# Moving twelve gate tiles from one attention stage to the next, and a branch one stage later

## The chip, the cores and the metric

The kernel runs on one core of a Trainium2 chip, as one program. A core has five engines that each take their own instructions in order: TensorE (matrix products), VectorE, ScalarE, GpSimd and SyncE, which here only starts transfers. They wait for each other on semaphores. The metric is the time of one execution in microseconds. Before the change it is 3099.02 us, the median of three runs (3095.4 to 3099.54).

## The reference

Two blocks follow each other. The first one (a recurrent branch, an attention with a learned selection, a mixture of experts) isn't touched. The second one runs two layers over 512 tokens of width 1024. What matters of a layer is this:

```
proj = x @ w_in[l]           # 3 x 512 for NA, 3 x 512 for DF, 384 + 256 + 32 for MLA, 3 x 1024 gate columns
na_out  = neighbourhood_attention(na_q, na_k, na_v, na_rpb[l])          # 8 heads of 64
df_out  = diff_attention(df_q, df_k, df_v, ...)                         # 4 heads, two score maps each
mla_out = latent_attention(m_cq, m_ckv, m_kr, w_mla_qb[l], w_mla_kvb[l], ...)   # 8 heads
    # inside: rms_norm(c_q), rms_norm(c_kv) over the 384 and 256 columns, then the products by w_qb and w_kvb
gates = sigmoid(gate_pre + b_gate[l])                                   # (512, 3, 1024)
merged = gates[:, 0] * (na_out @ w_branch[l, 0]) + gates[:, 1] * (df_out @ w_branch[l, 1]) \
       + gates[:, 2] * (mla_out @ w_branch[l, 2])
x = layer_norm(ALPHA * x + merged @ w_out[l]); x = layer_norm(ALPHA * x + ffn(x))
```

The gates depend on the layer's input alone; branch 0 needs na_out and its gates, branch 1 df_out, branch 2 mla_out.

## The kernel before

Every product with a weight is done in three matmuls: the weight block is loaded as `raw`, ScalarE casts it to a rounded copy `wh`, VectorE writes the rest `wl = raw - wh` (both in `split`, L145 and L146), and TensorE adds wh and wl products (`mmk`, L298, L299, L301). A tile of the class `FM` gives 128 output features of all 512 tokens in one PSUM accumulator `fm`; with 8 pieces of the input it takes 24 matmuls of 512 columns. There are four such accumulators (`mm`), three buffers for transposes and scores (`tr`) and one for the attention's output (`po`).

A gate (`gate`, L1638 ff.) is one such tile, a sigmoid on ScalarE (`bg`) and a store to DRAM (`t_d`); there are 3 x 8 in a layer. A branch (`branch`) has eight tiles of 12 matmuls; each multiplies its accumulator with a loaded gate (`tl`, L1656), and branches 1 and 2 add what the one before stored (`ml`, L1660 on GpSimd).

A layer goes through three attention stages. In each, `weave` interleaves two generators step by step, in the ratio of two numbers: an attention, whose chain of scores, softmax, transposes and products leaves TensorE idle, and a stream of independent work (the filler).

- NA stage: 16 units (`na_score`, `na_av`, `na_products`). A unit's scores are 4 matmuls (`nas`); VectorE adds the bias (L1589), takes the maximum (L1591, L1592), ScalarE does two sigmoids (L1595), VectorE scales (`naP`, L1601); one step later TensorE transposes (`napt`, L1607), the result is split, and again one step later come 12 products (`nao`). At each fourth unit two tiles project a head pair's queries and keys (`naq`, `nak`). Filler before: 20 gates.
- DF stage: 20 steps of scores (`dfs`), transposes (`dfpt`) and products (`dfo`), with a norm per head (a ones' matmul `dfm`). Filler before: four gates, the projection of the latent queries (`mcq`, four accumulators at once), one tile of branch 0, that of the latent keys (`mckv`, four accumulators), a tile of branch 0, the other six tiles, then the latent keys and values and the first half of the queries.
- MLA stage: 36 steps of scores (`ms`), transposes (`mpt`) and products (`mo`). Filler: the second half of the queries, branch 1.

Then branch 2 and the output projection. The functions `ev_cq` and `ev_ckv` empty the accumulators of the two latent projections: statistics on the PSUM tile by VectorE (`rms_stat`: bn_stats, then a root on ScalarE, L192, refined by VectorE), then a copy by ScalarE with that scale (L1762, L1778, and L1780 for the rotary columns). The root and the sigmoid come from different tables of ScalarE, and each change is a table load.

The order of instructions on each engine isn't quite that of the code: a scheduler of the framework moves them within what their dependences allow.

## Time and profile before

| | us |
|---|---|
| three runs, median | 3099.02 |
| profiled execution | 3100.77 |
| its span | 3098.6 |
| TensorE busy | 2908.0 (94%) |
| VectorE busy | 1840.3 (59%) |
| ScalarE busy | 1131.2 (37%) |

The span is the time from the first to the last instruction. TensorE's busy time is the sum of overlapping pipelined durations, so 94% doesn't mean that it is at its peak: what it loses shows in the spaces between the starts of its matmuls. In the profile PE is TensorE, PEld its loading of weights, DVE VectorE, ACT ScalarE, POOL GpSimd.

### The profile page before, as it was taken

Reading aid. Unit: us, or ns where it says so; the run is one execution under the profiler, and the core shown is the slowest. Engines: PE = TensorE matmul, PEld = TensorE weight load, DVE = VectorE, ACT = ScalarE, POOL = GpSimd, SP = SyncE. Lnnn points to the kernel's source line nnn. Section 1 sums busy time; section 2 is a strip of 40 time slices with the busy share of each in tenths; the row PEclk is TensorE's granted clock in tenths of the full one; section 3 lists DMA queues with packets and bytes.
Section 4 is the critical chain, followed back from the end, with each engine's and each line's share of the span. In section 5 each row is a group of like instructions: output and inputs, shape, how many; then the busy total and the mean of one; then the engine's idle time right before and its main releaser. Section 6 shows DMA issues by size and latency. Waiting matters only on the chain.

```text
span 3098.6 us, 36572 instructions
## 1 busy us (share of the span) xinstructions
PE 2908.0 (94%) x13749; PEld 2192.0 (71%) x13749; DVE 1840.3 (59%) x3521; ACT 1131.2 (37%) x1986; POOL 279.1 (9%) x263
## 2 busy tenths in 40 slices
PE   6988999979999989999999999999999999999998
PEld 5767777743333337888877888888878876788887
DVE  6899978543332347555788644425555589764434
ACT  4555244211000114444666322223444577432221
POOL 2133000310000001211002100000121000200000
PEclk9989999989999999999999999999999999999999
DMA  7222655769999984332244523334433233632341
GB/s 226 94 84 70 218 198 176 260 259 410 411 409 410 409 344 126 116 119 87 69 122 144 203 95 109 106 125 129 126 116 96 75 109 116 228 109 88 103 143 61
DMA packets 291648, 534.17 MB, mean 172 GB/s; under 512 B 29766, under 2 KB 172276, under 8 KB 287366
## 3 DMA queue, kind: packets, MB, share of 16 engines
q1 hardware_dynamic: 288872, 527.45, 48.9%
q0 software_dynamic: 2304, 4.20, 0.4%
q8 instruction: 110, 1.80, 0.2%
q14 instruction: 76, 0.62, 0.1%
q10 hardware_dynamic: 286, 0.09, 0.0%
HBM read 486.50 MB, written 44.38 MB: 171 GB/s over the span
## 4 chain that ended last, share of the span: by engine, by line
PE 57%; DMA 10%; DVE 6%; issue 3%; ACT 2%; POOL 1%; SPq 0%; DVEq 0%; POOLq 0%; ACTq 0%
PE fm L298 9%; PE fm L301 9%; PE fm L299 9%; DMA w<-in_moe_w_dram 6%; PE e L1385 5%; DMA w2r<-in_moe_w_dram 3%; PE ffo L301 2%; PE ffo L298 2%; PE ffo L299 2%; PE mix L298 1%; PE mix L299 1%; PE mix L301 1%; POOL tl L1660 1%; DVE wl L146 1%; PE cmb L1311 1%
## 5 line engine op out<-in xcount | busy, mean ns | idle before, releaser
L146 DVE TENSOR_TENSOR wl<-raw,wh 128x1024 fp32r<-128x1024 f32 (+3 forms) x403 | 461.8, 1147 | 317.2 <-ACT wh L145 315.8
L145 ACT CAST wh<-raw 128x1024 fp32r<-128x1024 f32 (+3 forms) x403 | 388.5, 966 | 546.5 <-PE fm L301 219.5
L298 PE MATMUL fm<-xT,wh 128*128 128x512 f32 (+1 forms) x1264 | 483.5, 385 | 0.0
L299 PE MATMUL fm<-xT,wl 128*128 128x512 f32 (+1 forms) x1264 | 481.4, 383 | 1.3 <-DVE wl L146 1.3
L301 PE MATMUL fm<-xT,wh 128*128 128x512 f32 (+1 forms) x1264 | 302.2, 381 | 0.0
L299 PEld LDWEIGHTS fm<-xT,wl 128*128 128x128 f32 x1264 | 239.5, 189 | 46.8 <-DVE wl L146 1.7
L298 PEld LDWEIGHTS fm<-xT,wh 128*128 128x128 f32 x1264 | 239.3, 189 | 45.2
L1385 PE MATMUL e<-w,xx 128*64 128x512 f32 x1024 | 256.8, 600 | 10.9 <-DMA w<-in_moe_w_dram 10.9
L301 PEld LDWEIGHTS fm<-xT,wh 128*128 128x128 f32 x1264 | 232.0, 188 | 45.6
L1385 PEld LDWEIGHTS e<-w,xx 128*64 128x64 f32 x1024 | 74.9, 137 | 157.9 <-issue 133.0
L1315 DVE TENSOR_TENSOR h<-h,cmb 128x512 f32<-128x512 f32 x128 | 80.7, 682 | 126.5 <-PE cmb L1314 126.1
L299 PE MATMUL fm<-uT,wl 128*128 128x512 f32 (+1 forms) x360 | 144.8, 402 | 3.8 <-DVE wl L146 3.8
L298 PE MATMUL fm<-uT,wh 128*128 128x512 f32 (+1 forms) x360 | 144.4, 402 | 0.0
L298 PE MATMUL ffo<-wl,hid 128*128 128x512 f32 x352 | 137.1, 390 | 0.0
L299 PE MATMUL ffo<-wh,hid 128*128 128x512 f32 x352 | 136.9, 389 | 0.0
L1385 PE MATMUL e<-w2r,hp 128*64 128x512 f32 x512 | 115.1, 596 | 10.1 <-ACT hp L1429 10.1
L1947 DVE SCALAR_TENSOR_TENSOR ffs<-ffs,fm 128x512 f32<-128x512 f32 x44 | 30.2, 687 | 139.3 <-ACT ffs L1946 139.3
L301 PE MATMUL ffo<-wh,hid 128*128 128x512 f32 x352 | 108.4, 389 | 0.0
L1949 DVE SCALAR_TENSOR_TENSOR ffs<-ffs,fm 128x512 f32<-128x512 f32 x44 | 30.2, 687 | 114.4 <-PE fm L301 114.4
L1660 POOL TENSOR_TENSOR tl<-ml,tl 128x512 f32<-128x512 f32 x32 | 47.7, 1496 | 555.1 <-DVE tl L1656 550.3
L1946 ACT ACTIVATE ffs<-fm 128x512 f32<-128x512 f32 x44 | 26.3, 598 | 188.7 <-PE fm L301 188.7
L1385 PEld LDWEIGHTS e<-w2r,hp 128*64 128x64 f32 x512 | 41.1, 136 | 73.1 <-issue 58.9
(603 smaller groups left out, 5938.0 us busy)
## 6 DMA issues: line engine op xcount, KB each, us to landing
w<-in_moe_w_dram SPq DMA_DIRECT2D x192, 512.0 KB
raw<-in_w_in_dram SPq DMA_DIRECT2D x71, 1024.0 KB
w2r<-in_moe_w_dram SPq DMA_DIRECT2D x128, 512.0 KB
raw<-in_w_ffn_in_dram SPq DMA_DIRECT2D x44, 1024.0 KB
w<-in_moe_w_dram SPq DMA_DIRECT2D x32, 1024.0 KB
raw<-in_w_mod_dram SPq DMA_DIRECT2D x42, 512.0 KB
raw<-in_w_ffn_out_dram SPq DMA_DIRECT2D x20, 1024.0 KB
raw<-in_w_out_dram SPq DMA_DIRECT2D x12, 1024.0 KB
```

Source lines behind the costliest of these rows:

```text
L145: S.copy(hi, src)
L146: (eng or V).tensor_tensor(lo, src, f(hi), OP.subtract)
L298: PE.matmul(ps, l[0], r[1], start=start and n == 0, stop=False)
L299: PE.matmul(ps, l[1], r[0], start=False, stop=False)
L301: PE.matmul(ps, l[0], r[0], start=False, stop=stop and n == len(pairs) - 1)
L1311: mm = PE.matmul(ps, pl, yl[:, cs], start=True, stop=False)
L1315: V.tensor_tensor(h1[i][m], h1[i][m], ps, OP.add)
L1385: mm = PE.matmul(ps[hs], lhs[:, hs], rhs[h], start=start, stop=stop)
L1660: G.tensor_tensor(th, m, th, OP.add)
L1946: S.activation(s, pgt, AF.Tanh, scale=0.5)
L1947: V.scalar_tensor_tensor(s, s, 1.0, pgt, OP.add, OP.mult)
L1949: V.scalar_tensor_tensor(s, s, 0.5, pup, OP.mult, OP.mult)
```

## The change

In both layers the NA stage keeps only the eight gates of branch 1. The other sixteen form a stream `rest`, of which four come first in the DF stage, two during each pause behind a latent projection, two between them and six behind them. Branch 0 goes into the MLA stage, ahead of branch 1. The two evacuations copy the accumulator first, and take the statistics and scale on the copy.

```diff
--- before.py
+++ after.py
@@ -1757,14 +1757,16 @@
             chat = []
 
             def ev_cq(i, ps):
-                r = rms_stat(ps, 384, 1e-6)
                 c = sg("cq", 384)
-                S.activation(c, ps, AF.Copy, scale=r)
+                S.copy(c, ps)
+                r = rms_stat(c, 384, 1e-6)
+                V.tensor_scalar(c, c, r, None, OP.mult)
                 chat.append(c)
 
             yield from dense_tm_g(xT, w_in2, 3072, 384, ev_cq, "mcq")
-            next(filler)
-            yield
+            for _ in range(2):
+                next(filler)
+                yield
             lat["cqT"] = affine_pages(chat, col["qng"][:, 3 * l:3 * l + 3], None, "cqT")
 
         def mla_project_kv(filler):
@@ -1773,15 +1775,17 @@
             lat0["krt"] = krt
 
             def ev_ckv(i, ps):
-                r = rms_stat(ps[:, 0:256], 256, 1e-6)
                 c = sg("ckv", 256)
-                S.activation(c, ps[:, 0:256], AF.Copy, scale=r)
+                S.copy(c, ps[:, 0:256])
+                S.copy(krt[:, i * 32:(i + 1) * 32], ps[:, 256:288])
+                r = rms_stat(c, 256, 1e-6)
+                V.tensor_scalar(c, c, r, None, OP.mult)
                 chat2.append(c)
-                S.copy(krt[:, i * 32:(i + 1) * 32], ps[:, 256:288])
 
             yield from dense_tm_g(xT, w_in2, 3456, 288, ev_ckv, "mckv")
-            next(filler)
-            yield
+            for _ in range(2):
+                next(filler)
+                yield
             lat["ckT"] = affine_pages(chat2, col["kvng"][:, 2 * l:2 * l + 2], None, "ckT")
             rope_rows(krt.rearrange("p (i h d) -> p i h d", i=4, h=1), 0, 16, rope16, 1, 0, 4)
             b = trp("krt")
@@ -1900,13 +1904,14 @@
                     mla_out.append(p)
 
         mT = []
-        weave((pipelined(16, na_score, na_av, 1), 17), (chain(gates(1, 0), gates(0, 16), gates(2, 8, range(4))), 20))
+        weave((pipelined(16, na_score, na_av, 1), 17), (gates(1, 0), 8))
         for _ in df_project():
             pass
-        br0 = branch(0, na_out, 16)
+        rest = chain(gates(0, 16), gates(2, 8))
         weave((pipelined(4, df_score, df_av), 20),
-              (chain(gates(2, 8, range(4, 8)), mla_project_q(br0), mla_project_kv(br0), br0, mla_kv(), mla_q(0)), 28))
-        weave((pipelined(8, mla_score, mla_av), 39), (chain(mla_q(1), branch(1, df_out, 0)), 10))
+              (chain((next(rest) for _ in range(4)), mla_project_q(rest), (next(rest) for _ in range(2)), mla_project_kv(rest), rest,
+                     mla_kv(), mla_q(0)), 36))
+        weave((pipelined(8, mla_score, mla_av), 39), (chain(mla_q(1), branch(0, na_out, 16), branch(1, df_out, 0)), 18))
         for _ in branch(2, mla_out, 8, mT):
             pass
 
```

What stands on TensorE in the NA stage of the first layer, before, between the scores of the seventh unit (`nas_10570`) and the transposes of the sixth (`napt_10589`); `fm_10536` is the second of two whole tiles that stand behind the sixth unit's own scores:

```order
L301 MATMUL fm_10536<-xT_9636,wh_10537 128x512
L301 MATMUL fm_10536<-xT_9637,wh_10537 128x512
L301 MATMUL fm_10536<-xT_9638,wh_10537 128x512
L301 MATMUL fm_10536<-xT_9639,wh_10537 128x512
L326 MATMUL nas_10570<-nak_10380,naq_10342 128x256
L327 MATMUL nas_10570<-nak_10380,naq_10341 128x256
L326 MATMUL nas_10570<-nak_10380,naq_10342 128x256
L327 MATMUL nas_10570<-nak_10380,naq_10341 128x256
L1607 MATMUL napt_10589<-ident,naP_10475 128x128 x4
```

And of the change, the same place, where the sixth unit (number 5, counted from 0) has the scores `nas_10361`, the seventh `nas_10406`, and `napt_10425` are the sixth unit's transposes:

```order
L326 MATMUL nas_10406<-nak_10280,naq_10242 128x256
L327 MATMUL nas_10406<-nak_10280,naq_10241 128x256
L298 MATMUL fm_10446<-xT_9632,wh_10447 128x512
L299 MATMUL fm_10446<-xT_9632,wl_10448 128x512
L298 MATMUL fm_10446<-xT_9633,wh_10447 128x512
L298 MATMUL nao_10433<-napt_10385,nav_9917 64x128
L1607 MATMUL napt_10425<-ident,naP_10377 128x128 x4
L299 MATMUL nao_10433<-napt_10385,nav_9917 64x128
```

Between the sixth unit's scores and its transposes stand, in place of whole tiles, the fifth unit's four transposes, twelve products, the seventh unit's four scores, three matmuls of a gate and one product.

What stands on ScalarE in the DF stage of the first layer, before, where the four tiles of the latent queries are emptied (`rsy` is a root, `cq` the copy with its scale):

```order
L192 ACT_TABLE_LOAD
L192 ACTIVATE rsy_12500<-msq_12497 128x1
L145 CAST wh_12708<-raw_12641 128x576
L1762 ACTIVATE cq_12506<-mcq_2540_12292,rst_12502 128x384
L192 ACTIVATE rsy_12515<-msq_12512 128x1
L1762 ACTIVATE cq_12521<-mcq_2541_12299,rst_12517 128x384
L192 ACTIVATE rsy_12530<-msq_12527 128x1
L1762 ACTIVATE cq_12536<-mcq_2542_12306,rst_12532 128x384
L192 ACTIVATE rsy_12545<-msq_12542 128x1
L145 CAST wh_12738<-raw_12736 128x576
L1762 ACTIVATE cq_12551<-mcq_2543_12313,rst_12547 128x384
```

And of the change, behind the four plain copies of the accumulators:

```order
L192 ACT_TABLE_LOAD
L192 ACTIVATE rsy_12072<-msq_12069 128x1
L1642 ACT_TABLE_LOAD
L1642 ACTIVATE bg_12158<-fm_12129,cols_2951 128x512
L192 ACT_TABLE_LOAD
L192 ACTIVATE rsy_12088<-msq_12085 128x1
L145 CAST pt_12188<-dfpt_12183 128x512
L145 CAST wh_12326<-raw_12257 128x1024
L192 ACTIVATE rsy_12104<-msq_12101 128x1
L1642 ACT_TABLE_LOAD
L1642 ACTIVATE bg_12224<-fm_12195,cols_2951 128x512
L192 ACT_TABLE_LOAD
```

The roots now stand among the sigmoids of two gates, with a table load at each change, and no copy stands behind a root. In the whole program ScalarE's listing has 57 table loads against 41.

## Rows read from the trace of the kernel before

**Rows 1.** Layer 1 by stage: us, busy PE, PEld, DVE, ACT, POOL (instructions), PEclk, DMA, GB/s

```profile
1196.00:1384.15 188.15, 181.23 (x995) 153.24 (x993) 100.86 (x164) 84.63 (x153) 37.12 (x46) 1.00 0.40 127
1453.50:1597.50 144.00, 136.26 (x679) 112.48 (x677) 110.67 (x290) 92.37 (x182) 0.00 (x0) 0.98 0.31 95
1597.50:1692.50 95.00, 89.84 (x454) 68.77 (x455) 85.82 (x207) 66.96 (x143) 11.37 (x9) 0.98 0.41 122
```

**Rows 2.** Chain that ended last: start, us, what; two successive tiles

```profile
1328.05 1.81 PE fm L301 x8
1333.49 1.81 PE fm L301 x8
```

**Rows 3.** TensorE around NA unit 13: start, us, engine, line, operation

```profile
1355.60 0.28 PE L327 MATMUL nas<-nak,naq 128*128 128x256 f32 x1
1355.72 0.60 PE L1607 MATMUL napt<-ident,naP 128*128 128x128 f32 x4
1356.08 0.30 PE L298 MATMUL nao<-napt,nav 128*64 128x128 f32 x1
...
1362.89 0.49 PE L1607 MATMUL napt<-ident,naP 128*128 128x128 f32 x3
```

**Rows 4.** TensorE's waits, NA stage: us in total, times, longest

```profile
PE nas L326 <- DVE nak L311: 6.3, 4, 1.9
```

**Rows 5.** Busy time, DF stage of layer 2

```profile
2416.90:2559.80 142.90, 135.22 (x678) 111.74 (x676) 110.49 (x289) 92.45 (x182) 0.00 (x0) 0.99 0.31 96
```

**Rows 6.** VectorE around NA unit 13

```profile
1355.99 0.69 DVE L1589 SCALAR_TENSOR_TENSOR nasm<-nas,nasm 128x512 f32<-128x512 f32 x1 [1.04 <-PE nas L327]
...
1357.32 1.22 DVE L146 TENSOR_TENSOR wl<-raw,wh 128x1024 fp32r<-128x1024 f32 x1
1358.45 0.16 DVE L1592 TENSOR_SCALAR mx<-mx 128x2 f32<-128x2 f32 x1
...
1360.04 1.25 DVE L1601 TENSOR_SCALAR naP<-nasm,su 128x256 f32<-128x256 f32 x2
```

**Rows 7.** ScalarE at the same place

```profile
1355.45 0.69 ACT L1642 ACTIVATE bg<-fm,cols 128x512 f32<-128x512 f32 x1 [1.48 <-PE fm L301]
1356.04 1.04 ACT L145 CAST wh<-raw 128x1024 fp32r<-128x1024 f32 x1
```

**Rows 8.** Stretches at a low granted clock (PEclk)

```profile
1532.20:1539.00 6.80, 5.34 (x13) 4.18 (x14) 5.79 (x29) 2.06 (x9) 0.00 (x0) 0.50 0.01 4
2214.90:2218.30 3.40, 3.40 (x13) 2.72 (x11) 3.04 (x5) 0.78 (x2) 0.00 (x0) 0.50 0.66 180
2262.70:2266.10 3.40, 3.40 (x16) 3.11 (x16) 2.74 (x3) 2.23 (x3) 0.00 (x0) 0.51 0.00 0
2498.20:2501.60 3.40, 3.40 (x9) 2.65 (x8) 2.63 (x15) 1.43 (x7) 0.00 (x0) 0.50 0.00 0
```

**Rows 9.** TensorE's waits, DF stage of layer 1

```profile
PE fm L298 <- ACT krt L1780: 3.8, 1, 3.8
PE dfo L298 <- DVE pt L146: 1.3, 2, 1.1
...
PE fm L298 <- ACT cq L1762: 0.2, 1, 0.2
```

**Rows 10.** Timeline about the latent key's copies, layer 1, and TensorE in layer 2

```profile
1528.57 1.28 ACT L1744 ACT_TABLE_LOAD   x1
...
1529.86 0.63 ACT L1744 ACTIVATE dfr<-dfsq 128x512 f32<-128x512 f32 x1
...
1533.06 0.47 ACT L1778 ACTIVATE ckv<-mckv,rst 128x256 f32<-128x256 f32 x1 [2.47 <-DVE rst L198]
...
2496.96 0.50 PE L298 MATMUL fm<-na_out,wh 128*128 128x512 f32 x1 [3.82 <-ACT krt L1780]
```

**Rows 11.** VectorE's groups of branch 0's tiles, DF stage, layer 1

```profile
L146 DVE TENSOR_TENSOR wl<-raw,wh 128x512 fp32r<-128x512 f32 x9 | 6.1, 685 | 2.2 <-ACT wh L145 2.2
...
L1656 DVE TENSOR_TENSOR tl<-tl,fm 128x512 f32<-128x512 f32 x8 | 5.4, 680 | 0.0
```

## The prediction

> **What bounds the kernel now.** I read the busy time of the stages of one layer first, then the chain of waits, then TensorE's waits stage by stage, then single stretches. In each stage of the attention part [rows 1] TensorE is the engine closest to full, so what counts is the time in which it issues nothing. A tile of 24 matmuls of 512 columns, one gate, starts 5.44 us after the one before it [rows 2], 0.227 us a matmul; the listed durations overlap, so a busy share says little and I count starts. In the neighbourhood (NA) stage, 188.15 us, there are 28 such tiles (152.3 us) and 16 units of scores, transposes and products, some 26 us by the starts in [rows 3]: about 10 us are lost, of which 6.3 are four waits at a new head pair [rows 4]. The differential (DF) stage, 144.0 us, holds some 127 us of issue: 17 lost. The latent (MLA) stage, 95.0 us, holds 82 (256 matmuls at 0.227, 160 transposes at about 0.1, 36 matmuls of 384 columns): 13 lost, and VectorE is busy for 85.82 of it. The second layer has the same stages [rows 5].
>
> The change adds and removes no matmul. Per layer it takes twelve gates (65.3 us of issue) out of NA, puts twelve into DF, takes branch 0 (8 x 12 matmuls, 21.8 us) out of DF and puts it into MLA: the issue sums to zero. The time changes by the holes alone: which close in DF and which open in NA and MLA.
>
> **NA stage: holes open.** Before, a gate tile lies in every step between a unit's scores and its transposes. I follow unit 13, which is an ordinary one. From the start of its last score matmul, at 1355.60 us, VectorE adds the bias at +0.39, reduces, splits a weight tile (1.22 us) at +1.72, scales the maximum at +2.85, and after two sigmoids on ScalarE writes the probabilities from +4.44 to +5.69 [rows 6, 7]; in quiet units the last step ends at +5.2. TensorE doesn't wait: the transposes come at +7.29 [rows 3], behind a gate of 5.44.
>
> Now only eight gates serve 17 steps. In the changed order unit 5 has no gate between: after its scores come unit 4's transposes (0.36 us), 12 products (0.8), unit 6's four score matmuls (0.47), three matmuls of a gate (0.7) and one product; then unit 5's transposes. That is about 2.4 us of work under a chain of 5.2, and TensorE takes its instructions in order: it stands 2.8 us. The chain is no shorter than before, since the same weight split stands in it (the order of VectorE there is unchanged). Units 9 and 13 are the same: 3 x 2.8 = 8.3. In units 0 and 1 the covers shrink to 6.3 and some 3 us plus waits: 2.4 lost (0.6 and 1.8). At the end units 14 and 15 have no gate behind them, only six matmuls of the next projection: 2.5 us before the last transposes, 0.8 before the last products. Together 13.9 us per layer, 27.8 for both. Bounds: 0 if the chain always ran beside something; 5.2 us in each of eight bare steps, 42 per layer, if nothing did. I take 13.9, worked from the order.
>
> **The clock in these holes.** The granted clock follows such stops at times: of the six waits of about 2 us at a new head pair (three in each layer), two in the second layer were followed by 3.4 us at half clock (1.2 GHz) [rows 8], each worth 1.7 us with TensorE working. With eight new holes of 2.5 to 3 us, at one in three: 4.5 us. Bounds: 0 and 8 x 1.7 = 13.6. The Trainium skill (TensorE: Matmul & The Clock Gate, HAM oscillation — how this bites in real kernels) says that a loop which waits in every turn lets the gate fall in every turn; by that the term is 13.6 instead of 4.5. The trace agrees only in part, two of six. A product that splits each hole in two of about 1.4 us speaks for the lower number.
>
> **DF stage: a hole closes.** The projection of the latent key holds all four accumulators until ScalarE has copied them out with a scale that comes from bn statistics on the PSUM tile, through VectorE, a table load, the root and back. The next tile waits 3.8 us for it, and so in the second layer [rows 9, 10]. In between VectorE does the norm of a differential head, which is why it is late. Behind it the clock was halved, 6.8 us in the first layer (TensorE working for 5.34) and 3.4 in the second [rows 8]: 2.7 + 1.7. The change copies first and computes the statistics from the copy, so the copy needs nothing from VectorE. After the projection's last matmul come two pairs of scores and transposes before the next tile, and copies of 0.5 us are done by then. What goes: 2 x 3.8, 4.4 and 2 x 0.2 (the small wait behind the query projection [rows 9]), 12.4 us. What is late next is nothing, unless ScalarE is. Bounds: 8 (the waits alone) to 24 (the 17 lost in each layer, less 5 that I leave to the tail and the steps between scores and tiles).
>
> The cost put on ScalarE: twelve gates more in each layer's DF stage, 1.04 + 0.69 each [rows 7], 21 us, and table loads of 1.28 us [rows 10], since the four roots and the gates' sigmoids now alternate (the second pair of listings in the section on the change): 8 more per layer, 10.3 us. ScalarE was busy for 92.37 of 144 us [rows 1] and would be for at most 124 of 181; a gate's sigmoid waits for TensorE anyway. I cost it at nothing. If each of the 16 loads stood in the path it would be 20.5 us. The eight scalings per layer that move to VectorE hide likewise: it was busy for 110.67 of 144 us [rows 1] and gains 12 weight splits of 1.22 us [rows 6] while it loses branch 0's 11 us, so its share falls to some 65%.
>
> The Trainium skill (ScalarE: Activation LUTs, What ACT_TABLE_LOAD costs) gives 1283 ns for the load and about 1380 more for a drain, 2.66 us a switch; by that the upper end would be an estimated 42.6 us instead of 20.5. The load agrees with the trace; behind it no drain shows, for the root begins 0.01 us after the load ends [rows 10].
>
> **DF tail.** The last four steps run without filler, because the filler stream has 30 pieces for a pace of 36. The waits there (1.3 us at the products [rows 9]) stay and the transposes of the first latent head lose some: I put 0, from -2 to +4.
>
> **MLA stage: filler doubles.** Branch 0 costs VectorE 0.69 + 0.68 us a tile [rows 11], 11 us, so 96.8 in all; TensorE holds 104 us of issue. Both are near full now and each step is a chain between them. I take the loss of 13 as unchanged but for 1 us per layer: 2. Bounds: -13 per layer (all holes filled) to +5 (0.3 us in each of the 16 pairs of steps).
>
> **Sum.** 27.8 + 4.5 - 12.4 + 0 + 2 = +21.9. The profiled execution took 3100.77 us (span 3098.6), 1.75 above the median of the three; so 3122.7 for its like, and 3099.02 + 21.9 = 3121 us against the median.
>
> **Rivals.**
> Filler fills holes (faster): in DF and MLA the added tiles are just what TensorE lacked, and the stages lose next to nothing. My sum leaves some 11 and 14 us per layer there. For it: the NA stage with 20 fillers lost 5%. Against: MLA's VectorE would be at 93%. The point from which it decides is a loss in both together of under 15 instead of 25 per layer; with 11, 3121 - 28 = 3093, with 8, 3087; I put it at 3090.
> The holes stay small (no change): units 5, 9 and 13 find their probabilities earlier because VectorE has four fewer weight splits before them: without the split in the chain 1.2 us less at each and half at the ends: -7 per layer, and no half clock: 3121 - 14 - 4.5 = 3102.
> The clock falls each time (slower yet): 13.6 instead of 4.5, 3130; with MLA at its upper bound 3138.
> ScalarE in the path: table loads before a gate's sigmoid keep an accumulator; at half of 20.5, 3131.
>
> **Chances.** Forecast 0.52; clock or MLA or ScalarE worse 0.18; holes small 0.14; filler fills holes 0.16. About 0.2%, 6 us, is what a measurement of this kernel can tell from no change. Faster 0.16, same 0.14, slower 0.70. The likeliest case alone spans 3109 to 3131; the range that leaves out 2 in 10 reaches into both sides, 3091 to 3134.
>
> **What would show it.** Right: in the NA stage TensorE waits for the probabilities' line (unit 13 doesn't now [rows 3]) by 5 to 12 us per layer; the stage takes about 138 us per layer against 188 less 65; no wait of TensorE for the copy of the latent key; the DF stage about 181 and the MLA stage about 118. Wrong: an NA stage under 130 us, an MLA stage under 110, or a DF stage over 188.

## The result and the profile after

The changed kernel takes 3136.44 us (median of 4, 3133.97 to 3140.28) beside 3099.28 for the one before (3095.4 to 3099.75): a ratio of 1.0122, interval 1.0107 to 1.0136. It is slower, by 37 us, as forecast in sign and by 15 us more than in size (3121, and just above the range). Its profiled span is 3138.5 us against 3098.6.

The stages of the first layer, from the start of the first scores of one to that of the next, with the projection between NA and DF and branch 2 behind MLA as rows of their own; the columns are as in [rows 1], which started the NA stage 13 us earlier:

```profile
1207.73:1339.62 131.89, 112.09 (x618) 93.25 (x619) 78.46 (x140) 58.16 (x117) 29.25 (x40) 0.92 0.29 93
1339.62:1414.07 74.45, 71.89 (x355) 59.03 (x353) 35.47 (x64) 29.35 (x46) 10.43 (x16) 1.00 0.24 74
1414.07:1592.70 178.63, 175.58 (x870) 147.54 (x869) 119.52 (x297) 117.42 (x206) 0.00 (x0) 0.99 0.31 94
1592.70:1705.27 112.57, 109.97 (x549) 86.90 (x548) 96.30 (x220) 73.14 (x151) 11.41 (x9) 0.98 0.49 150
1705.27:1730.40 25.13, 22.49 (x98) 17.89 (x96) 13.48 (x20) 7.40 (x12) 11.07 (x8) 1.00 0.83 273
```

The NA stage of the kernel before, cut in the same way, first layer and second, and then that of the change in the second:

```profile
1209.61:1384.15 174.54, 168.35 (x938) 142.88 (x938) 95.02 (x157) 79.78 (x147) 32.73 (x40) 1.00 0.38 123
2169.74:2347.46 177.72, 171.54 (x938) 145.49 (x938) 96.42 (x157) 79.62 (x147) 31.54 (x40) 0.98 0.38 120
2186.47:2318.73 132.26, 113.16 (x618) 94.36 (x619) 78.41 (x140) 58.26 (x117) 29.71 (x40) 0.91 0.29 93
```

What to see: the granted clock of the NA stage fell to 0.92 (1.00 before), and no other stage of the first layer shows that. In the second layer it is 0.91 (0.98 before), and the projection behind it fell to 0.96 (1.00 before).

To compare stages that hold different work I take from each length the issue, the matmuls that started in it at their full-clock distances (0.227 us for 512 columns, 0.171 for 384, 0.131 for 288, 0.118 for 256, 0.060 for 128, 0.109 for a transpose). What is left is lost time. Each cell has the first and the second layer, in us; the last column is the time at half clock (a granted clock of 0.50, 1.2 instead of 2.4 GHz) within the first two stages. Each row comes from the one profiled execution of its kernel; that of d16_gates was the slowest of its four, 11 us above their median. In warm and bias_and_filled the useless products that they add count as issue, 12.7 and 10.0 us per layer:

| kernel | NA and projection | DF | MLA | branch 2 | at 1.2 GHz |
|---|---|---|---|---|---|
| before | 9.1, 12.3 | 17.3, 16.4 | 12.9, 12.9 | 1.2, 1.0 | 0, 6.8 |
| after | 36.7, 40.0 | 8.6, 8.4 | 9.1, 10.5 | 3.3, 3.5 | 20.4, 30.6 |
| e1_copies | 11.0, 10.8 | 17.4, 20.2 | 14.2, 12.9 | 1.1, 0.9 | 3.4, 3.4 |
| e2_moves | 35.8, 38.0 | 19.2, 18.2 | 8.7, 8.7 | 2.4, 2.8 | 20.4, 27.2 |
| d16_gates | 24.6, 19.5 | 23.6, 23.7 | 8.6, 10.4 | 2.7, 2.6 | 17.0, 10.2 |
| half_gates | 27.5, 27.9 | 8.0, 9.1 | 10.4, 10.4 | 2.6, 2.4 | 13.6, 10.2 |
| warm | 25.3, 27.0 | 8.3, 8.5 | 10.5, 10.4 | 2.4, 3.5 | 6.8, 10.2 |
| branch0_back | 36.6, 37.3 | 6.7, 6.5 | 13.4, 12.0 | 1.0, 1.0 | 20.4, 23.8 |
| early_keys | 2.9, 3.9 | 17.3, 16.4 | 12.8, 12.9 | 1.1, 0.9 | 0, 0 |
| halves_16 | 15.8, 20.0 | 21.7, 20.3 | 12.4, 12.4 | 1.3, 0.9 | 3.4, 6.8 |
| early_bias | 32.3, 33.0 | 8.5, 8.5 | 10.5, 9.0 | 2.2, 2.9 | 20.4, 23.8 |
| keys_and_bias | 20.9, 18.1 | 9.0, 7.5 | 10.6, 8.7 | 2.9, 2.2 | 10.2, 6.8 |
| before_keys_order | 3.1, 3.0 | 9.7, 9.7 | 12.9, 13.0 | 1.0, 0.9 | 0, 0 |
| bias_and_filled | 21.3, 19.3 | 7.5, 7.9 | 8.6, 10.4 | 2.1, 2.1 | 6.8, 6.8 |

From before to after NA and projection lose 55.3 us more in both layers, DF 16.7 less, MLA 6.3 less, branch 2 loses 4.6 more, the stages behind it take 4.9 more, and the program up to the NA stage was 1.9 us shorter: +39.9, the difference of the spans. So the NA stage and its projection lose more than the whole difference. In the DF stage the time at half clock was 6.8 and 3.4 us before, 2.8 and 1.6 after, 6.8 and 13.7 in e1_copies, 10.2 and 6.8 in e2_moves, 13.7 and 13.9 in d16_gates, 13.3 and 9.2 in halves_16, and nothing in before_keys_order. TensorE's waits there, in the first layer (who waited for whom, us in total, times, longest), answer to [rows 4]:

```profile
PE napt L1607 <- DVE naP L1601: 9.0, 6, 4.0
PE nao L298 <- ACT naof L1629: 6.6, 3, 2.2
PE nas L326 <- DVE nak L311: 6.3, 4, 1.9
PE nao L298 <- DVE napt L146: 0.7, 1, 0.7
```

Before, only the third was there (6.3 us) and 0.6 us of the first. The stretches at half clock in the same stage, with the columns of [rows 8], where the first layer had none:

```profile
1231.20:1234.60 3.40, 3.40 (x11) 2.71 (x10) 2.11 (x7) 1.68 (x5) 0.00 (x0) 0.54 0.00 0
1255.10:1261.90 6.80, 6.30 (x25) 4.99 (x26) 5.48 (x9) 1.73 (x6) 2.75 (x4) 0.52 0.00 0
1292.70:1296.10 3.40, 3.40 (x18) 2.92 (x17) 1.26 (x2) 0.59 (x1) 0.08 (x1) 0.53 0.76 290
1316.60:1320.00 3.40, 3.40 (x15) 2.82 (x14) 3.30 (x6) 0.71 (x2) 0.00 (x0) 0.53 0.00 0
1330.20:1333.60 3.40, 3.40 (x18) 2.82 (x16) 1.13 (x2) 0.57 (x1) 0.07 (x1) 0.54 0.72 277
```

How a stop and the clock go together, on TensorE at unit 9's transposes (timeline: start, duration, in brackets the idle time and who ended it):

```profile
1289.38 0.39 PE L298 MATMUL fm<-xT,wh 128*128 128x512 f32 x1
1291.97 0.27 PE L298 MATMUL nao<-napt,nav 128*64 128x128 f32 x1 [2.20 <-ACT naof L1629]
1292.08 0.70 PE L1607 MATMUL napt<-ident,naP 128*128 128x128 f32 x4
...
1293.56 0.73 PE L299 MATMUL fm<-xT,wl 128*128 128x512 f32 x1
1294.09 0.63 PE L298 MATMUL fm<-xT,wh 128*128 128x512 f32 x1
```

The gate's matmuls that came 0.23 us apart come 0.4 to 0.5 us apart behind the stop.

In the DF stage TensorE no longer waits for the latent key's copy, 3.8 us in [rows 9]; what is left of waits is this:

```profile
PE dfo L298 <- DVE pt L146: 1.9, 2, 1.6
PE dfm L1741 <- ACT dfsq L1734: 1.2, 2, 0.7
```

### The profile page after: what moved, and what is told of

Read it like the earlier page. It is cut to its first block, busy times and chain, and to the rows that moved or that the text cites. A ratio compares the mean times of both kernels' runs of the same rounds, so it can differ in the third digit from the quotient of the medians.

```text
span 3138.5 us, 36589 instructions
## 1 busy us (share of the span) xinstructions
PE 2924.3 (93%) x13749; PEld 2205.8 (70%) x13749; DVE 1840.9 (59%) x3537; ACT 1154.6 (37%) x2002; POOL 279.0 (9%) x263
## 5 line engine op out<-in xcount | busy, mean ns | idle before, releaser
L146 DVE TENSOR_TENSOR wl<-raw,wh 128x1024 fp32r<-128x1024 f32 (+4 forms) x403 | 456.2, 1133 | 293.1 <-ACT wh L145 291.7
L145 ACT CAST wh<-raw 128x1024 fp32r<-128x1024 f32 (+4 forms) x403 | 388.4, 965 | 543.6 <-PE fm L301 220.1
L299 PE MATMUL fm<-xT,wl 128*128 128x512 f32 (+1 forms) x1264 | 491.9, 391 | 1.3 <-DVE wl L146 1.3
L298 PE MATMUL fm<-xT,wh 128*128 128x512 f32 (+1 forms) x1264 | 492.3, 392 | 0.0
L301 PE MATMUL fm<-xT,wh 128*128 128x512 f32 (+1 forms) x1264 | 306.8, 385 | 0.0
L298 PEld LDWEIGHTS fm<-xT,wh 128*128 128x128 f32 x1264 | 244.7, 194 | 46.9 <-issue 0.5
L301 PEld LDWEIGHTS fm<-xT,wh 128*128 128x128 f32 x1264 | 234.0, 190 | 47.4 <-issue 1.0
```

The costliest lines, as they stand in the source:

```text
L145: S.copy(hi, src)
L146: (eng or V).tensor_tensor(lo, src, f(hi), OP.subtract)
L298: PE.matmul(ps, l[0], r[1], start=start and n == 0, stop=False)
L299: PE.matmul(ps, l[1], r[0], start=False, stop=False)
L301: PE.matmul(ps, l[0], r[0], start=False, stop=stop and n == len(pairs) - 1)
```

## The experiments

The theory at the start: the NA stage with eight covers in 17 steps makes the loss, by stops and by the clock behind them, and the copies give back some 12 us. Rivals: branch 0 beside the latent attention makes it; the copies are worth nothing; the stops alone count and the clock doesn't.

**The two halves of the change.** e1_copies is the kernel before with the new `ev_cq` and `ev_ckv`, one filler per pause as it was (the diff shows the first of the two functions). e2_moves is the changed kernel with the old ones.

```diff
-                r = rms_stat(ps, 384, 1e-6)
                 c = sg("cq", 384)
-                S.activation(c, ps, AF.Copy, scale=r)
+                S.copy(c, ps)
+                r = rms_stat(c, 384, 1e-6)
+                V.tensor_scalar(c, c, r, None, OP.mult)
```

> The kernel before with one part of the change alone: the query and key latents are copied out of the accumulators first, and their statistics and scaling follow on the copy. Theory (the copies return time, the moves cost it): the 3.8 us wait for the latent-key copy and the 0.2 us one go in each layer and with them the half clock behind them, some 11 us in all: 3088, ratio 0.9963. Rival (the wait is not on the path, or another takes its place): 3097 to 3100. The two VectorE scalings per tile may delay the norms of the differential heads: then above 3100.

> The changed kernel with the old evacuation of the latents (statistics from the accumulator, a scaled copy out): the moves alone. Theory: the two parts add up, so 3136.5 + 8 to 12 = 3145 to 3149. Rival: in the changed kernel the wait is hidden (a gate more lies between), and it stays at 3136 to 3138; then the whole slowdown is of the moves and the copies are worth nothing there.

Measured: e1_copies 3102.58 us, 1.0016 (1.0006 to 1.0025); e2_moves 3158.73, 1.0201 (1.0182 to 1.0221). Both theories of mine fell here; e1_copies came out as its last case ("above 3100"), e2_moves above both of its own. Alone, the copies gain nothing, they lose 5 us; in the moved order they are worth 22. TensorE's waits in the first layer's DF stage of e1_copies say why nothing is gained; the first five rows:

```profile
PE dfo L298 <- DVE pt L146: 2.6, 3, 1.3
PE dfs L326 <- ACT dfP L1507: 1.4, 1, 1.4
PE dfpt L1514 <- DVE pt L146: 1.4, 1, 1.4
PE krt L1791 <- DVE krt L1530: 1.3, 1, 1.3
PE dfm L1741 <- ACT dfsq L1734: 0.7, 1, 0.7
```

The wait of 3.8 us is gone, and four of 1.3 to 1.4 have come, for VectorE or for ScalarE behind it: TensorE runs ahead to the latents' transposes and to the next scores, and VectorE still has the same statistics to do. That layer's DF stage takes as long as before (143.87 us, 143.77 before). The loss shows in the second layer's, which has the same waits but 13.7 us at half clock instead of 3.4, half of which more is 5.1; beside [rows 5]:

```profile
2415.39:2562.06 146.67, 137.58 (x678) 114.47 (x676) 111.22 (x297) 91.38 (x182) 0.00 (x0) 0.95 0.30 93
```

In e2_moves it is the other way round: gates lie there, but the copies wait for the statistics, 5.9 us of ScalarE's time in the first layer, and the scores wait for ScalarE's softmax. That the one makes the other is my reading of these waits:

```profile
PE dfm L1741 <- DVE pt L146: 2.4, 1, 2.4
PE dfo L298 <- DVE pt L146: 2.1, 3, 1.6
PE dfs L326 <- ACT dfP L1507: 1.9, 1, 1.9
PE fm L298 <- ACT cq L1762: 1.4, 1, 1.4
```

**More gates in the NA stage.** d16_gates keeps sixteen there.

```diff
-        weave((pipelined(16, na_score, na_av, 1), 17), (gates(1, 0), 8))
+        weave((pipelined(16, na_score, na_av, 1), 17), (chain(gates(1, 0), gates(0, 16)), 16))
-        rest = chain(gates(0, 16), gates(2, 8))
+        rest = gates(2, 8)
...
-              (chain((next(rest) for _ in range(4)), mla_project_q(rest), (next(rest) for _ in range(2)), mla_project_kv(rest), rest,
-                     mla_kv(), mla_q(0)), 36))
+              (chain((next(rest) for _ in range(4)), mla_project_q(rest), mla_project_kv(rest), rest,
+                     mla_kv(), mla_q(0)), 28))
```

> The changed kernel, but eight of the gates that it moves stay beside the neighbourhood attention (16 there instead of 8, 8 beside the differential attention instead of 16); branch 0 stays beside the latent attention and the copies come first. Theory (the loss is made by the neighbourhood stage with too few covers): the holes of some 18 us per layer and the 20 to 31 us at half clock go, so 3136.5 - 2 x 22 to 2 x 27 = 3083 to 3092. Rival (the loss is made by branch 0 beside the latent attention and what VectorE then owes at branch 2): at most 10 us come back, 3126 or more. Second rival (what the neighbourhood stage gains the differential stage loses, for lack of its eight gates): about 3110.

Measured: 3131.87, 1.0110 (1.0093 to 1.0127). The time lies in the first rival's range, but the stages don't bear that rival out. The NA stage recovers 12 and 20 us, though it still stops 4.2 us at unit 1 with 6.8 us at half clock behind it, but the DF stage now loses 23.6 instead of 8.6. This is the second rival's mechanism, and more of it than that said: eight gates are missed where they were taken from.

**The same eight gates in smaller pieces.** half_gates issues each gate as two pieces of 12 matmuls.

```diff
...
+                mmk(ps, pairs[:4], True, False)
+                yield
+                mmk(ps, pairs[4:], False, True)
...
-        weave((pipelined(16, na_score, na_av, 1), 17), (gates(1, 0), 8))
+        weave((pipelined(16, na_score, na_av, 1), 17), (half_gates(1, 0), 16))
```

> The changed kernel, with the same eight gates beside the neighbourhood attention, each issued as two pieces of 12 matmuls in two of the 17 steps, so that every step but one has a cover of 2.7 us instead of every second one 5.4. The work of each stage is as in the changed kernel. Theory A (what hurts is that whole steps stand bare, and that the clock falls in their stops): most stops shrink below 1 us and the half clock goes, 3096 to 3110. Theory B (eight gates are too few however they are laid: a chain of 5.2 us stands under each step): every step now stops for some 1 to 2 us, the sum of the stops is about the same, and the time is 3130 to 3140.

Measured: 3116.67, 1.0069 (1.0049 to 1.0089), between the two. In the first layer's NA stage TensorE waits for the probabilities as long as in the changed kernel (9.0 us in six places there):

```profile
PE napt L1607 <- DVE naP L1601: 9.1, 9, 2.6
```

27 us less are spent at half clock (23.8 instead of 51.0 in both layers), and the projection stage is as long as before the change. I took that for the clock's effect alone, but the 6.6 us that the changed kernel lists under naof are gone too, and they are stops at the same transposes (shown under bias_and_filled). So stops and half clock both shrank here, and this run can't tell what each is worth.

**Useless work in the stops.** warm adds matmuls that nobody reads.

```diff
         def na_av(u, _):
+            if u in (0, 1, 5, 9, 13, 15):
+                ws = mmp("warm")
+                for _ in range(16 if u == 1 else 8):
+                    tc.keep_in_program_order(PE.matmul(ws, xT[0][:, 0, 0:128], xT[0][:, 0], start=True, stop=True))
```

> The changed kernel with useless products added into its new holes: 8 matmuls of 512 columns ahead of the transposes of units 0, 5, 9, 13 and 15 and 16 ahead of unit 1's, in a scrap accumulator that nobody reads; 56 per layer, 12.7 us of issue by the 0.227 us of a matmul. Theory (a large part of the loss is the half clock behind the stops, 20.4 us of the neighbourhood stage in the first layer and 30.6 in the second): the stops are filled, the clock stays, and the time falls although work is added, by 15 to 25: 3112 to 3122. Rival (the stops themselves are the loss, the clock costs nothing in them): nothing is gained, and where a product outlasts its stop something is lost: 3136 to 3146.

Measured: 3143.69, 1.0148 (1.0131 to 1.0165), as the rival had it. The time at half clock fell from 51.0 to 17.0 us, and the two stages took as long as without the 12.7 us of useless work (207.7 and 209.3 us instead of 206.3 and 209.5): the work was free there (1.1 of the 5 us by which the span grew lie in these stages), but the clock gave nothing. Two things spoiled the test. The added accumulator made the scheduler put unit 1's gate behind its transposes, so real cover was lost there. And the stop before unit 10's transposes grew (1.6 us by the starts, 0.9 in the changed kernel), where a gate partly at half clock had hidden more of its late start. VectorE in the changed kernel, at unit 10, shows what is late:

```profile
1297.50 0.69 DVE L1589 SCALAR_TENSOR_TENSOR nasm<-nas,nasm 128x512 f32<-128x512 f32 x1 [3.37 <-POOL nasm L1588]
```

The scores stand ready at 1288.9 us, and VectorE waits for GpSimd's bias tile. GpSimd had waited for its load:

```profile
1296.02 2.83 POOL L1588 TENSOR_TENSOR nasm<-nab,colmask 128x256 f32<-128x256 f32 x4 [17.79 <-DMA nab<-Bd]
```

And that load stands on SP's queue behind a gate's store, which waits for the sigmoid, and a weight load of 1 MB, which waits for VectorE's split to free its buffer:

```profile
1287.68 0.34 SPq L1647 DMA_DIRECT2D t_d<-bg  x1
1290.07 0.37 SPq L400 DMA_DIRECT2D raw<-in_w_in_dram  x1
1290.55 0.45 SPq L1574 DMA_DIRECT2D nab<-Bd  x1
```

**The bias ahead in the queue.** early_bias is the changed kernel with the next head's bias loaded behind the last use of the one before, into a buffer of its own taken from a shared ring (that line is left out here).

```diff
...
-                nP["bt"] = sa("nab")
-                load(nP["bt"], Bd[l * 8 + h])
+                if u == 0:
+                    nP["bt"] = t_([128, 512], F32, "BT", "nab")
+                    load(nP["bt"], Bd[l * 8])
...
                 G.tensor_tensor(s3[:, m], bv, colmask[:, n].unsqueeze(1).to_broadcast([128, 8, 32]), OP.add)
+            if n2 and h < 7:
+                nP["bt"] = t_([128, 512], F32, "BT", "nab")
+                load(nP["bt"], Bd[l * 8 + h + 1])
```

> The changed kernel with one thing moved: the bias of the next head is loaded behind the last use of the one before (a buffer of its own, taken from the seven of the scratch ring), ahead of the gate's store and of a weight load on SP's queue. In the changed kernel VectorE waits 8.5 us in three places of the first layer's neighbourhood stage for GpSimd's bias tile, and GpSimd for the load: unit 10's scores stand ready at 1288.9 us and its bias lands at 1296.0. Theory (with bare steps the chain of a unit begins with the bias, and the load's place in the queue is in the path): 3 to 8 us per layer come back, 3120 to 3130. Rival (those chains have time anyway): 3133 to 3139.

Measured: 3125.68, 1.0094 (1.0077 to 1.0110), as the theory had it: 11 us back by the medians, 9 by the ratios to the kernel before (whose intervals overlap a little), and NA and projection lose 11 us less in the table. VectorE's wait for the bias (8.5 us in the first layer) is gone. Before the change VectorE had waited 5.8 us for it there too, but TensorE, with a gate in every step, waited only 0.6 us for the probabilities. At units 5, 9 and 13 the stops even grew, from 2.4 to 2.7 to 2.9 us by the starts, and the stops that remain are these, in the first layer's NA stage and the start of the projection:

```profile
PE nao L298 <- ACT naof L1633: 7.9, 3, 2.8
PE nas L326 <- DVE nak L311: 6.3, 4, 1.9
PE napt L1611 <- DVE naP L1605: 4.2, 5, 2.2
PE nao L298 <- DVE napt L146: 0.7, 1, 0.7
```

**The clock again.** bias_and_filled adds useless products to that kernel, written into the transposes' own accumulator (which is then overwritten), and leaves units 0 and 1 alone.

```diff
             b = trp("napt")
+            if u in (5, 9, 13, 15):
+                for _ in range(12 if u < 15 else 8):
+                    tc.keep_in_program_order(PE.matmul(b, xT[0][:, 0, 0:128], xT[0][:, 0], start=True, stop=True))
```

> The kernel of early_bias with useless products in its remaining stops: 12 matmuls of 512 columns (2.7 us) ahead of the transposes of units 5, 9 and 13 and 8 (1.8 us) ahead of unit 15's, into the transposes' own accumulator, which is overwritten; the start of the stage, where the run named warm had also moved a gate, is left alone. TensorE's order is otherwise that of early_bias, but for three matmuls of a gate that stood in the stops of units 5, 9 and 13 and now come behind them (0.7 us each, 2 us per layer). Theory (behind the stops the half clock costs, 20.4 and 23.8 us of the two layers' stages, half of it lost): the clock stays in most of them, 7 to 10 us per layer come back less these 2: 3125.7 - 10 to - 16 = 3110 to 3116. Rival (what the clock takes, the next wait for the probabilities gives back): 3125 to 3131.

Measured: 3120.38, 1.0070 (1.0053 to 1.0087): 5.3 us faster than early_bias with 88 matmuls more (7 us by the ratios, whose intervals overlap). It lies between the theory and the rival. With the transposes' accumulator filled first, the same stops are put down to the probabilities, and naof is gone from the list. NA and projection together got 3.7 us shorter in the second layer and 1.0 in the first, where unit 1 had to wait for its bias again, 1.7 us more. The second layer, first early_bias, then bias_and_filled, NA stage alone:

```profile
2178.68:2303.81 125.13, 109.72 (x621) 92.82 (x622) 78.03 (x139) 57.68 (x116) 32.13 (x40) 0.93 0.30 97
```

```profile
2178.92:2307.34 128.42, 116.70 (x694) 98.37 (x694) 82.41 (x146) 60.40 (x123) 31.48 (x40) 0.98 0.30 97
```

The NA stage grew by 3.3, for it now contains the end's wait and 10 us of useless work; the projection behind it fell from 77.5 to 70.5. In both layers the time at half clock fell from 44.2 to 13.6 us. The 30.6 us, of which half would be lost at two matmuls' time for one, gave back 5 to 7 us and the 4 that the gates' three matmuls cost behind each stop (at units 5, 9 and 13 a wait of 0.7 to 1.3 us is left behind the useless products): by this estimate about 10 of 15. So the half clock is a real loss, and perhaps a third of it would have been waiting anyway; with one pair of kernels and overlapping intervals the share is rough.

**Branch 0.** branch0_back puts it behind the sixteen gates of the DF stage.

```diff
-        rest = chain(gates(0, 16), gates(2, 8))
+        rest = chain(gates(0, 16), gates(2, 8), branch(0, na_out, 16))
...
-                     mla_kv(), mla_q(0)), 36))
+                     mla_kv(), mla_q(0)), 44))
-        weave((pipelined(8, mla_score, mla_av), 39), (chain(mla_q(1), branch(0, na_out, 16), branch(1, df_out, 0)), 18))
+        weave((pipelined(8, mla_score, mla_av), 39), (chain(mla_q(1), branch(1, df_out, 0)), 10))
```

> The changed kernel with branch 0 back beside the differential attention, behind the sixteen gates there; beside the latent attention only branch 1, as before. The neighbourhood stage is as in the changed kernel. Theory (branch 0 beside the latent attention saves some 3 us per layer there and costs some 4.6 behind it, where VectorE is late for branch 2 and for the stages after; in the differential stage it costs no more than its own 21.8 us): 3136 less 2 to 6 per layer, 3124 to 3132. Rival (in the latent stage it is covered work, in the differential stage there is no room left): 3138 to 3146. The neighbourhood stage's loss, about 33 us per layer, doesn't move under either.

Measured: 3131.58, 1.0106 (1.0089 to 1.0122), as the theory had it, at its upper end: 5 us, with intervals that overlap. DF, MLA and branch 2 of its first layer:

```profile
1414.55:1613.07 198.52, 195.93 (x966) 165.04 (x965) 130.39 (x313) 121.86 (x214) 0.00 (x0) 1.00 0.37 116
1613.07:1708.18 95.11, 88.98 (x453) 68.47 (x452) 85.09 (x202) 66.67 (x142) 11.29 (x9) 0.98 0.41 120
1708.18:1730.96 22.78, 22.21 (x98) 17.83 (x96) 16.25 (x22) 8.07 (x13) 9.68 (x7) 1.00 0.72 238
```

The DF stage is 19.9 us longer for 21.8 us of issue; MLA and branch 2 are back at their lengths of before. In the changed kernel VectorE comes late out of the MLA stage, which shows at branch 2 and the output projection behind it:

```profile
PE mix L298 <- DVE tl L1656: 2.6, 1, 2.6
PE fm L299 <- DVE wl L146: 1.4, 1, 1.4
PE mix L298 <- DVE wl L146: 1.4, 1, 1.4
```

**The waits at a new head pair.** early_keys is the kernel before with the projection of a pair two units earlier.

```diff
-                if h % 2 == 0:
-                    na_qk(h // 2)
+                if u == 0:
+                    na_qk(0)
+                if h % 2 and h < 7:
+                    na_qk(h // 2 + 1)
```

> The kernel before, with the query and key projection of a head pair issued two units earlier (at the second head of the pair before it), so that its pages are ready when the scores ask for them. Theory (a stop of TensorE in the neighbourhood stage costs its length, and the half clock behind some): the three waits of about 2 us in each layer go, 12 us, and the two stretches at half clock in the second layer, 3.4: 3098 - 12 to - 16 = 3082 to 3086. Rival (the wait is only moved: VectorE's chain of the unit before is as late as the key page): 3094 to 3100.

Measured: 3081.35, 0.9943 (0.9926 to 0.9961), the theory's case and just past its range. Of [rows 4] the first layer keeps the 0.7 us at its start, and the clock stays at 2.4 GHz through both NA stages:

```profile
1207.67:1375.90 168.23, 167.13 (x929) 142.21 (x930) 95.56 (x158) 78.83 (x147) 31.64 (x40) 1.00 0.39 126
2159.88:2329.16 169.28, 167.16 (x930) 142.21 (x930) 95.72 (x158) 78.82 (x147) 31.21 (x40) 1.00 0.39 125
```

keys_and_bias does this and early_bias in the changed kernel.

> The changed kernel with the bias loaded early as in early_bias, and the query and key projection of a head pair two units early as in early_keys. Theory (in a stage of bare steps each of these waits is in the path, and the 48 matmuls of the projection, moved two units up, cover a step that stood bare): the three waits of 2 us per layer go as they did in the kernel before (17 us there), and some of the stops at the units that now have a cover: 3095 to 3112. Rival (the chains of 5.2 us only stop TensorE elsewhere): 3115 to 3125.

Measured: 3103.98, 1.0024 (1.0012 to 1.0036), the theory's case. With the moves as they were, a fifth of the slowdown against the kernel before is left. But the early keys help that kernel too: against early_keys, which has them without the moves, the moves still cost 25 us by the ratios. The NA stage still loses 21 and 18 us, in the first layer mostly in three waits for the probabilities (6.9 us) and one for the accumulator's copy (2.7).

**Two ways to share the covers.** halves_16 has sixteen gates in 32 pieces in the NA stage, eight gates and then branch 0 in the DF stage.

```diff
...
-        weave((pipelined(16, na_score, na_av, 1), 17), (gates(1, 0), 8))
+        weave((pipelined(16, na_score, na_av, 1), 17), (chain(half_gates(1, 0), half_gates(0, 16)), 32))
...
-        rest = chain(gates(0, 16), gates(2, 8))
+        rest = chain(gates(2, 8), branch(0, na_out, 16))
...
-        weave((pipelined(8, mla_score, mla_av), 39), (chain(mla_q(1), branch(0, na_out, 16), branch(1, df_out, 0)), 18))
+        weave((pipelined(8, mla_score, mla_av), 39), (chain(mla_q(1), branch(1, df_out, 0)), 10))
```

> Sixteen gates beside the neighbourhood attention, each in two pieces (32 pieces for 17 steps), eight gates and branch 0 beside the differential attention, branch 1 alone beside the latent attention, copies first: each of the two stages gets its cover. Theory (each step needs about 5 us of other work beside its chain, and the loss is what is missing): the neighbourhood stage loses 10 to 15 us per layer (before 8 and 12, changed 33), the differential stage 9 to 13 (before 17, changed 8.5), nothing is lost behind: 3085 to 3096. Rival (the halves are the harm or the differential stage gains nothing): 3105 or more.

Measured: 3121.22, 1.0079 (1.0062 to 1.0096), the rival's case: the NA stage does better than in d16_gates in the first layer, but DF loses more than before the change, with twice the gates, 3.8 us of it where the key's transposes wait for VectorE. My reading is that the gates are used up ahead of the latents, and branch tiles, which need VectorE themselves, lie behind.

before_keys_order turns that round in the kernel before: early keys, copies first, branch 0's tiles first and the last four gates behind the latents.

```diff
...
-        br0 = branch(0, na_out, 16)
+        br0 = chain(branch(0, na_out, 16), gates(2, 8, range(4, 8)))
-              (chain(gates(2, 8, range(4, 8)), mla_project_q(br0), mla_project_kv(br0), br0, mla_kv(), mla_q(0)), 28))
+              (chain((next(br0) for _ in range(4)), mla_project_q(br0), mla_project_kv(br0), br0, mla_kv(), mla_q(0)), 28))
```

> The kernel before with the early query and key projection, the copies first, and branch 0's tiles ahead of the last four gates in the differential stage, so that gates, which need no statistics of VectorE, lie behind the latent key. Theory (in e1_copies the 3.8 us wait came back as waits of the latent transposes for VectorE's statistics, because what lay behind was branch tiles; sixteen gates there left 8.5 us lost): the differential stage loses 8 to 13 us instead of 17, so 3081 less 8 to 18 = 3063 to 3073. Rival (VectorE's work is the limit whatever lies there): 3079 to 3087.

Measured: 3069.75, 0.9912 (0.9896 to 0.9929), as the theory had it, and the fastest of all: 25 us under the kernel before on the same chip. NA, DF and MLA of its first layer, at full clock throughout:

```profile
1208.99:1377.47 168.48, 167.56 (x935) 142.57 (x936) 95.20 (x157) 79.15 (x147) 31.53 (x40) 1.00 0.40 127
1447.06:1583.20 136.14, 131.87 (x678) 111.07 (x676) 113.15 (x297) 91.85 (x182) 0.00 (x0) 1.00 0.32 98
1583.20:1677.83 94.63, 87.72 (x452) 66.94 (x453) 85.83 (x206) 66.54 (x142) 11.38 (x9) 1.00 0.40 121
```

The DF stage holds the same work as before, in 136.1 us instead of 143.8. Against early_keys the kernel is 10 us faster by the ratios, so the copies and the four gates moved behind the latents pay together. No run has this order with the old copies, so the share of each is not shown.

## Why the prediction was right or wrong

The sign and the place were right: the NA stage loses more than DF and MLA gain. The size was not. The stages' lengths show where: DF 178.6 us (181 forecast) and MLA 112.6 (118) came out shorter than said, and the NA stage shrank by 42.7 us in the first layer instead of 50 (188 to 138; with the 13.6 us ahead of the first scores that [rows 1] counts it is 145), with 4.9 more in the projection behind it.

- **Holes in the NA stage, 27.8 forecast.** The places are those named, and the sizes are about right once the bias is there in time: in early_bias units 5, 9 and 13 stop for 2.74, 2.91 and 2.74 us by the starts (2.8 forecast), the end for 2.33 and 0.84 (2.5 and 0.8); units 0 and 1 stop for 1.45 and 0.51 (0.6 and 1.8), near in sum alone. In the changed kernel itself the new stops add up to 34 us in both layers. What I did not see is the load of the bias: I read the chain from the scores on, in a unit whose bias had long been there, and so had a term at nothing that cost 9 to 11 us with the clock behind it (early_bias); unit 1 alone stopped for 4.1 and 3.8 us. TensorE's wait for the probabilities' line was to be 5 to 12 us per layer, and is 9.0. But at units 5, 9 and 13 the profile of the changed kernel names ScalarE's copy of the output accumulator (naof) instead; that copy and the probabilities end within some 0.1 us of each other there, and in bias_and_filled, where the transposes stand first, the same stop is put down to the probabilities. With these three it is 15.6 us, more than I said.
- **The clock, 4.5 forecast: the step that failed.** I put a fall behind one stop in three, from two of six waits of 2 us. The two layers together spend 51.0 us of these stages at half clock against 6.8, in five and seven stretches, some of double length: behind each of the eight new stops of over 2 us, behind three of the six old waits, and behind one of the two stops of 1.9 us at the end. Counted at half their length that is 22 us more, where I had 4.5, and this with the bias makes up the miss in the NA stage: 55.3 - 22 leaves 33 of holes. bias_and_filled makes it an estimate that about two thirds of such a count are really lost; the rest is time in which the next chain would have been waited for. The Trainium skill (TensorE: Matmul & The Clock Gate, HAM oscillation — how this bites in real kernels) describes a loop that loses the clock in each turn, by waits for DMA that are longer than most stops here. I had weighed that rule and set it aside for a sample of six. This case's trace agrees with it in the changed kernel, and for shorter stops; it doesn't in every kernel, for in keys_and_bias only five of ten stops of 2.3 to 2.9 us had half clock behind them.
- **DF stage, -12.4 forecast.** -16.7 measured, for a reason that I had only half. The copies first, by themselves, don't return the wait (e1_copies: +5); in the moved order, where gates lie behind them, they do (e2_moves against the changed kernel: 22 us). "What is late next is nothing" was wrong: VectorE was late next, as soon as TensorE could run on.
- **ScalarE at nothing.** Right: it was busy for 117.42 us of 178.63 (at most 124 of 181 forecast), and TensorE's waits for it in that stage are 1.2 us.
- **MLA stage, +2 forecast.** It gained 6.3, but VectorE carried its lateness over: 4.6 more in branch 2, which I had not looked at, and 1.5 in the stretch behind the first layer's. So the sum came near the forecast by luck. branch0_back, 5 us faster without branch 0 there, gives the worth of the place: 5 us lost against the DF stage. In the stretch behind the second layer's branch 2 the time varies from kernel to kernel (its loss was 14.4 us before, 17.3 in branch0_back and 17.1 in before_keys_order). Most of these 3 us goes with the clock: that stretch has 6.5 us at half clock before and 11.1 and 11.0 in those two, 2.3 more when counted at half. Why it falls there stays open.
- **Rivals.** "The clock falls each time", with an MLA stage at its bound, came to 3138 and was nearest, though MLA had no part in it: by luck the late bias stood in for it. "Filler fills holes" is half true: DF and MLA together lose 17.7 and 18.9 us, between the 25 of my sum and the 15 that it asked for, and what they gain is smaller than the loss in NA. "The holes stay small" fell with the stops of 2.4 us at units 5, 9 and 13.

## What to carry to other kernels

Before moving independent work out of a stage, lay what remains against the length of the chain in each step, with all that the chain begins with: also the loads, by their place in an in-order queue behind stores and loads that wait for other engines. Price a stop of TensorE with the half clock behind it, in every turn, until a run shows less. In these runs a wait on an accumulator that was removed came back at the next instruction that needed the same late engine, unless work without that engine stood right behind it.

## What was not expected of the hardware

- The 1 MB weight load and the 256 KB bias behind it on SP's queue: the bias, issued at 1290.55 us, was used from 1296.02 on, 5.5 us later. Issuing it ahead of them, into a buffer of its own, moved the kernel by 9 to 11 us (early_bias).
- Useless matmuls in the stops made the NA and projection stages no longer, or hardly (1 us in both layers for 25 us of work in warm, 5 us less for 20 in bias_and_filled), and kept the clock in most of them: 34 us less at 1.2 GHz with 112 of them (warm), 31 us less with 88 (bias_and_filled).
- The same edit has either sign: the copies lose 5 us in one order of TensorE's work and gain 22 in another.
